# A two-layer diffusion step: the modulation products of VectorE over 512 inputs per instruction instead of 256

## The chip, the cores and the metric

The kernel runs on one core of one Trainium2 chip. Its time is the device time of one execution in microseconds (us); the time before is the median of three runs. The engines of a core are TensorE (PE), VectorE (DVE), ScalarE (ACT), GpSimd (POOL) and SyncE (SP); each works through its own list of instructions in order, and semaphores hold an instruction until what it needs is there.

## The reference, cut to what matters

Two layers run over 640 tokens: 128 context tokens and 512 latent ones, of width 2048. Each layer computes

```
shift, scale, gate = silu(cond) @ ada_w[l] + ada_b[l]     # cond: c_ctx or c, 2048 wide
h   = x * (1 + scale) + shift
z   = h @ w_in[l]                                          # 6656 wide, 52 tiles of 128
mix = [attention * silu(ag), hgrn2 * silu(hgate), silu(LN(conv)) * silu(cgate)]
x   = LayerNorm(ALPHA * x + gate * (mix @ w_out[l]))
```

`cond` is one vector for the context tokens and another for the latent ones, so each of the 3 x 2048 modulation values of a layer is needed twice. The change concerns `silu(cond) @ ada_w`, and in it the four parts that VectorE computes: the gate of layer 0, and scale, shift and gate of layer 1.

## The kernel before, in words

The matrix products run on TensorE in fp32r, with each operand split into a high and a low part. A layer takes the 52 column tiles of `w_in` one after the other (`NTILES`, line 35: 16 tiles of the recurrence, 4 of its gate, 12 of attention, 8 of the convolution (`cb`, `ca`), then 8 of `ag`, tiles 40 to 47, and 4 of `cgate`, tiles 48 to 51). Each tile's product lands in one of two PSUM buffers `z` (the list `ZP`), and is fetched from there by a generator of its own, which hands the buffer back (`zput`). After the tiles come five column groups of `w_out` and the layer norm.

The order of all instructions is written out by the program itself. The loop over the tiles (line 1254) emits the matmuls of a tile in four chunks and calls `pump(3, rate)` twice in each, eight times a tile. `pump` (line 260) adds `rate` to a credit, spends each whole credit on one step of the modulation (`pump_ada`), and then lets the generators in `active` take up to three steps, in the order of the list. A step is what a generator emits up to its next `yield`; one that can't get a buffer yields `BLOCK`, and that counts as no step. The rates of layer 0 are 1.0 for tiles 3 to 19, 0.85 for 20 to 31, 0.5 for 32 to 44 and 1.2 for 45 to 51 (`RATE`, line 74); in the first four groups of `w_out`, twelve pumps each give 4/3. Layer 1 gives 0.5, 0.5, 0.0 and 0.8.

`pump_until(cond)` (line 277) emits until a condition holds: it gives one step to the generators, and when all of them are blocked, one step to the modulation. Before each tile it waits in this way for a free `z` (line 1255); before the last group of `w_out` it waits until no modulation of layer 0 is left (line 1470).

`S` (line 142) is a list of nine scratch buffers of 128 x 688, from which nearly everything takes its working space; a buffer given back goes to the end of the list. Those that matter here:

- `ada_dve` (line 337), the modulation. A part is 8 blocks of 256 inputs; a block takes 8 tiles of weights (128 x 512, `raw`, three of them on the way) and one `S` buffer with both conditioning rows of that block, fetched from `crow` in DRAM and spread over all partitions. The buffer of the next block is taken in the middle of a block (`q == 4`), that of the finished block goes back at its end. One step holds two products of 256 inputs (`dve.scalar_tensor_tensor` with `accum_out`).
- `e_ca` (line 1009 on) leaves the convolution's result of its four tiles in one `S` buffer each.
- `conv_ln` (line 1035), the layer norm over the convolution. It starts when the four results are there and attention is done, takes two buffers (`r`, `r2`), emits sums, waits five steps, and takes two more for each of two column sums (`summed`, line 1050: `hi, lo = yield from S.getn(F32R, F32R)`). It gives the four results and `r2` back after the first column sum, and at its end sets the flags `("mix", l, 12)` to `("mix", l, 15)`.
- `e_gate` (line 1094) takes one buffer, writes silu of its `z` into it, gives `z` back, then waits for the flag of its part of `mix`. For the four `cgate` tiles this is the flag of `conv_ln`.

`getn` (line 112) takes several buffers at once, and takes none until all are free.

Of the kernel before, what the change touches and what calls it, by code (L numbers as in the profile page):

```python
# [9 lines left out]
F32 = mybir.dt.float32  # L10
F32R = mybir.dt.float32r
BF16 = mybir.dt.bfloat16
U8 = mybir.dt.uint8
AF = mybir.ActivationFunctionType
ALU = mybir.AluOpType
AX = mybir.AxisListType

P = 128
D = 2048
KT = 16  # L20
# [52 lines left out]
ADAD = [(0, 2), (1, 1), (1, 0), (1, 2)]  # L73
# [52 lines left out]
def trunk(ctx: ExitStack, tc: tile.TileContext, A: dict):  # L126
    nc = tc.nc
    act, dve, pool, pe, sync = nc.scalar, nc.vector, nc.gpsimd, nc.tensor, nc.sync
# [3 lines left out]
    drp = ctx.enter_context(tc.tile_pool(name="drp", bufs=1, space=bass.MemoryType.DRAM))  # L132
    ctx.enter_context(tc.manual_schedule())

    def new(name, shape, dt=F32):
        return sb.tile(shape, dt, name=name)
# [5 lines left out]
    S = Slots(sb, "s", 9, SLOT)  # L142
# [6 lines left out]
    cmask = new("cmask", [P, 4 * 32], U8)  # L149
    Zd = Slots(sb, "zd", 1, 4 * 160)  # L150
    sm = new("sm", [P, SMW])
    junk = new("junk", [P, 256], BF16)
    aacc = new("aacc", [P, 8, 32])
    nsink = new("nsink", [P, 16])
    oml = new("oml", [P, 2, 4])
    lbt = new("lbt", [P, 2, 2, 4])
# [9 lines left out]
    mb = [psp.tile([P, 512], F32, name=f"m{i}") for i in range(4)]  # L166
    ZP = Free(zt)
    M = Free(mb)
    crow = drp.tile([8, 2, 256], F32, name="crow")
    gsc = drp.tile([2, 2, D], F32, name="gsc")  # L170
    n0 = drp.tile([T, D], F32, name="n0")

# [43 lines left out]
    pool.memset(scs[:, 0:512], 0.0)  # L216
    act.activation(scond[:, :, 0:2], sm[:, SM["cond"]:SM["cond"] + 32].rearrange("p (k c) -> p k c", c=2), AF.Silu)
    crs = S.take()
    sync.dma_start(out=crs[0:16, 0:256], in_=A["condr"])
    act.activation(crs[0:16, 0:256], crs[0:16, 0:256], AF.Silu)  # L220
    pool.dma_start(out=crow.rearrange("a c k -> (a c) k"), in_=crs[0:16, 0:256])
    S.put(crs)

    def zput(z):
# [70 lines left out]
    def adab(l, part):  # L295
        o = SM["adab"] + 48 * l + 16 * part
        return sm[:, o:o + 16]
# [38 lines left out]

    def ada_dve(l, part):
        pi = ADAD.index((l, part))
        rows, fly = deque(), deque()
        tiles = [(kb, q) for kb in range(8) for q in range(8)]  # L340
        nrow = nxt = 0
        for kb, q in tiles:
            while nxt < len(tiles) and len(fly) < (HF if hold else FL):
                if fly and len(RAW.f) <= KEEP[0]:
                    break
                r = yield from RAW.get()
                sync.dma_start(out=r, in_=A["adawD"][pi, tiles[nxt][0], tiles[nxt][1]])
                fly.append(r)
                nxt += 1
            if nrow <= kb or (nrow <= min(kb + 1, 7) and q == 4):  # L350
                t = yield from S.get()
                sync.dma_start(out=t[:, 0:512], in_=crow[nrow].rearrange("c k -> (c k)").partition_broadcast(P))
                rows.append(t)
                nrow += 1
            yield
            r = fly.popleft()
            for n in range(2):
                if n:
                    yield
                for c in range(2):  # L360
                    o = 2 * (2 * q + n) + c
                    dve.scalar_tensor_tensor(junk, r[:, 256 * n:256 * n + 256], 1.0, rows[0][:, 256 * c:256 * c + 256],  # L362
                                             op0=ALU.mult, op1=ALU.mult, accum_out=aacc[:, kb, o:o + 1])
            RAW.put(r)
            if q == 7:
                S.put(rows.popleft())
        yield
        b = adab(l, part).unsqueeze(2).to_broadcast([P, KT, 2])
        t = yield from S.get()
        gT = t[:, 32:64].rearrange("p (c k) -> p c k", c=2)  # L370
        dst = (shf, scl)[part][l] if part < 2 else gT.rearrange("p c k -> p k c")
        dve.tensor_reduce(t[:, 0:32], aacc.rearrange("p a x -> p x a"), axis=AX.X, op=ALU.add)
        dve.scalar_tensor_tensor(dst, t[:, 0:32].rearrange("p (k c) -> p k c", c=2), float(part % 2), b,
                                 op0=ALU.add, op1=ALU.add)
        if part == 2:
            yield
            yield
            yield
            b2 = yield from M.get()
            pe.transpose(b2[0:32, 0:128], t[:, 32:64], ident)  # L380
            act.copy(t[0:32, 128:256], b2[0:32, 0:128])
            M.put(b2)
            act.dma_start(out=gsc[l].rearrange("c (k p) -> (c k) p", p=P), in_=t[0:32, 128:256])
        S.put(t)
        flags.add(("ada", l, part))
# [832 lines left out]
    for l in range(DEPTH):  # L1218
        if l == 0:
            adaq.extend([ada_dve(0, 2), ada_dve(1, 1), ada_dve(1, 0)])  # L1220
        else:
            adaq.append(ada_dve(l, 2))
# [196 lines left out]
        for gi, (n0c, w) in enumerate(GROUPS[:-1]):  # L1419
# [4 lines left out]
            for k0 in range(0, KT, 2):  # L1424
                for tts, k in [(p, k) for p in ((range(3), range(3, TT)) if k0 == 0 else (range(TT),))
                               for k in (k0, k0 + 1)]:
                    hi, lo = osp[l, gi, k // kper]
                    o = w * (k % kper)
# [47 lines left out]
        for tt in range(TT):  # L1476
            b = banks.popleft() if last else obank[tt]
            for k in range(KT):
                hi, lo = osp[l, gi, k // 2]
                o = w * (k % 2)  # L1480
# [50 lines left out]
def pack(i):  # L1531
    f = np.float32
    ac = np.ascontiguousarray
    a = {}
    xs = np.concatenate([i["x_prompt"][0], i["x_sample"][0]], 0)
    a["xr"] = ac(xs)
    a["xT"] = ac(xs.reshape(T, KT, P).transpose(2, 1, 0))
    w = np.asarray(i["w_in"])
    cols = np.concatenate([np.arange(OFF[n] + 128 * j, OFF[n] + 128 * j + 128) for n, j in NTILES])
    w = w[:, :, cols].reshape(DEPTH, 4, 4, P, NN, P)  # L1540
    a["win"] = ac(w.transpose(0, 4, 1, 3, 2, 5)).reshape(DEPTH, NN, 4, P, 512)
    wo = np.asarray(i["w_out"])
    tiles = []
    for n0c, wd in GROUPS:
        kper = 512 // wd
        t = wo[:, :, n0c:n0c + wd].reshape(DEPTH, KT // kper, kper, P, wd)
        tiles.append(t.transpose(0, 1, 3, 2, 4).reshape(DEPTH, KT // kper, P, 512))
    a["wout"] = ac(np.concatenate(tiles, 1))
    aw = np.asarray(i["ada_w"])
    a0 = aw[0].reshape(4, 4, P, 3, 8, 256)[:, :, :, 0:2]  # L1550
    a["adaw0"] = ac(a0.transpose(3, 4, 0, 2, 1, 5)).reshape(2, 8, 4, P, 1024)
    ad = np.stack([aw[l][:, D * p:D * p + D].reshape(8, 256, 8, 2, P) for l, p in ADAD])
    a["adawD"] = ac(ad.transpose(0, 1, 3, 5, 4, 2)).reshape(4, 8, 8, P, 512)
    a["lnw_r"] = ac(i["ln_w"])
    a["lnb_r"] = ac(i["ln_b"])
    a["ckT"] = ac(np.asarray(i["cache_k"])[0].transpose(0, 3, 2, 1)).reshape(DEPTH, P, 256)
    a["cv"] = ac(i["cache_v"][0]).reshape(DEPTH, P, 256)
    a["st"] = ac(np.asarray(i["state_hgrn"])[0].transpose(0, 3, 1, 2, 4))
    s = np.zeros((P, SMW), f)

    def put(n, v):
        v = np.asarray(v).reshape(P, -1)
        s[:, SM[n]:SM[n] + v.shape[1]] = v

    def ch(v, n):
        return np.asarray(v).reshape(DEPTH, n, P).transpose(2, 0, 1)

    put("lb", np.asarray(i["hg_lower_bounds"]).reshape(2, DEPTH, 4, P).transpose(3, 0, 1, 2))
    put("normw", ch(i["hg_norm_w"], 4))
    put("convw", np.asarray(i["conv_w"]).reshape(DEPTH, TAPS, 4, P).transpose(3, 0, 2, 1))  # L1570
    put("convb", ch(i["conv_b"], 4))
    put("clnw", ch(i["conv_ln_w"], 4))
    put("clnb", ch(i["conv_ln_b"], 4))
    put("lnw", ch(i["ln_w"], KT))
    put("lnb", ch(i["ln_b"], KT))
    put("sink", np.broadcast_to(np.asarray(i["attn_sink"]).reshape(1, 16), (P, 16)))
    cond = np.stack([np.asarray(i["c_ctx"]), np.asarray(i["c"])[0]], -1)
    put("cond", cond.reshape(KT, P, 2).transpose(1, 0, 2))
    put("adab", np.asarray(i["ada_b"]).reshape(DEPTH, 3, KT, P).transpose(3, 0, 1, 2))
    a["condr"] = ac(cond.T.reshape(2, 8, 256).transpose(1, 0, 2)).reshape(16, 256)  # L1580
    a["small"] = s
    a["ident"] = np.eye(P, dtype=f)
    p = np.arange(P)
    t = np.arange(512)
    inv = (np.float32(10000.0) ** (-np.arange(32, dtype=f) / np.float32(32))).astype(f)
    pos = np.where((p < 64)[:, None], (t // 64)[None], (t % 64)[None]).astype(f)
    ang = (pos * inv[p % 32][:, None]).astype(f)
    a["cos"] = np.cos(ang).astype(f)
    a["sin"] = (np.sin(ang) * np.where((p % 64) < 32, -1, 1)[:, None]).astype(f)
    m = np.zeros((P, 640), f)  # L1590
    b = np.arange(P)
    m[:, 128:256] = np.where(b[None] >= p[:, None], 0, NEG)
    m[:, 384:512] = np.where(b[None] <= p[:, None], 0, NEG)
    a["amask"] = m
    si = (p % 32)[:, None]
    ti = np.arange(32)[None]
    same16, same8 = (si // 16 == ti // 16), (si // 8 == ti // 8)
    cm = np.stack([~same16, same16 & ~same8, same8 & (ti >= si), same8 & (ti <= si)], 1)
    a["cmask"] = cm.reshape(P, 128).astype(f)
    return a  # L1600
# [20 lines left out]
```

## Time and profile before

| | |
|---|---|
| median of 3 runs | 2241.13 us (2240.1 to 2241.21) |
| the profiled execution | 2247.12 us, span 2245.3 us |
| TensorE busy | 2177.4 us (97%) |
| VectorE busy | 1457.9 us (65%) |
| ScalarE, GpSimd busy | 1144.7 us, 601.9 us |
| mean granted TensorE clock | 0.994 of full speed |

The span runs from the first instruction to the last; the profiled execution is 6 us above the median of the runs. Layer 0 takes the tiles from about 120 to 934 us, then `w_out` to about 1160 us; layer 1 follows in the same way. A busy TensorE is not TensorE at its peak, since matmuls are pipelined and their ends are modelled.

### The profile page before, as it was taken

The numbers are of one execution on the slowest core, as the hardware profiler recorded it, in microseconds if no ns is written. First come the engines' busy times: TensorE is split into PE (matmuls) and PEld (weight loads), VectorE is DVE, ScalarE is ACT, GpSimd is POOL, SyncE is SP. The second block draws the span as 40 slices with busy tenths as digits, with TensorE's granted clock in tenths as the row PEclk, the third lists the DMA queues.
The fourth block names the chain that finished last, engine by engine and source line by source line (L and its number), as shares of the span: only waits on it lengthen the run. The fifth ranks groups of instructions, "written<-read, shape, count | busy, mean of one in ns | idle before, by whom it ended". The sixth has DMA issues, their size and how long they took to land.

```text
span 2245.3 us, 42128 instructions
## 1 busy us (share of the span) xinstructions
PE 2177.4 (97%) x15854; PEld 2076.1 (92%) x15854; DVE 1457.9 (65%) x3799; ACT 1144.7 (51%) x2051; POOL 601.9 (27%) x690
## 2 busy tenths in 40 slices
PE   5899999999999999999989999999999999999997
PEld 2699999999999999988989999999999999998887
DVE  2478899557669999766673666543654779225457
ACT  1267877546565435511155787774555543462112
POOL 0033344332222343300032344433222123331003
PEclk9999999999999999999999999999999999999999
DMA  9978787897766888964426777778776576676333
GB/s 358 392 206 199 185 209 182 201 219 173 176 159 155 206 193 212 259 233 128 128 108 158 156 172 162 162 173 189 160 163 137 110 173 147 150 164 212 99 99 123
DMA packets 210557, 403.61 MB, mean 180 GB/s; under 512 B 24656, under 2 KB 30512, under 8 KB 209712
## 3 DMA queue, kind: packets, MB, share of 16 engines
q1 hardware_dynamic: 138992, 271.85, 38.4%
q0 software_dynamic: 61440, 116.96, 30.2%
q10 hardware_dynamic: 9920, 12.10, 1.7%
q8 instruction: 124, 2.03, 0.4%
q14 instruction: 81, 0.66, 0.1%
HBM read 383.46 MB, written 12.11 MB: 176 GB/s over the span
## 4 chain that ended last, share of the span: by engine, by line
PE 75%; DVE 9%; DMA 6%; issue 5%; ACT 3%; POOL 1%; ACTq 1%; SPq 0%; POOLq 0%; DVEq 0%
PE z L1175 29%; PE z L1173 19%; PE z L1431 9%; PE m L1431 8%; DVE junk L362 4%; DMA x<-adaw 2%; PE m L948 2%; PE m L1482 2%; PE m L862 1%; DMA s<-xT 1%; PE m L916 1%; DMA s<-s 1%; DMA wh<-win 1%; PE m L664 1%; ACT s L1391 1%
## 5 line engine op out<-in xcount | busy, mean ns | idle before, releaser
L1175 PE MATMUL z<-HH,wh 128*128 128x384 f32 x3296 | 1046.6, 339 | 0.0
L1173 PE MATMUL z<-HH,wh 128*128 128x256 f32 x3296 | 926.6, 283 | 1.9 <-DMA wh<-win 1.0
L292 POOL DMA_DIRECT2D wh<-win x388 | 345.2, 936 | 1095.3 <-ACT wh L291 1024.0
L1173 PEld LDWEIGHTS z<-HH,wh 128*128 128x128 f32 x3296 | 619.5, 189 | 5.8 <-DVE wh L287 1.6
L1175 PEld LDWEIGHTS z<-HH,wh 128*128 128x128 f32 x3296 | 620.6, 188 | 1.5
L1175 PE MATMUL z<-HL,wh 128*128 128x384 f32 x1648 | 558.2, 339 | 0.0
L362 DVE SCALAR_TENSOR_TENSOR junk<-raw,s 128x256 bf16<-128x256 f32 x1024 | 502.5, 491 | 53.2 <-DMA raw<-adawD 25.0
L1173 PE MATMUL z<-HL,wh 128*128 128x256 f32 x1648 | 461.6, 280 | 0.0
L1173 PEld LDWEIGHTS z<-HL,wh 128*128 128x128 f32 x1648 | 310.9, 189 | 0.0
L1175 PEld LDWEIGHTS z<-HL,wh 128*128 128x128 f32 x1648 | 310.4, 188 | 0.0
L291 ACT ACTIVATE wh<-wh 128x512 fp32r<-128x512 f32 x400 | 253.0, 633 | 78.5 <-PE z L1175 67.4
L290 ACT CAST wh<-raw 128x512 fp32r<-128x512 f32 x400 | 244.0, 610 | 72.0 <-issue 36.1
L286 ACT CAST wh<-raw 128x512 fp32r<-128x512 f32 x136 | 83.0, 621 | 305.0 <-PE m L1431 153.8
L1027 DVE SCALAR_TENSOR_TENSOR s<-s,sm,s 128x655 f32<-128x655 f32 x240 | 229.6, 957 | 6.3
L1431 PE MATMUL z<-wh,HH 128*128 128x512 f32 (+1 forms) x640 | 182.1, 368 | 0.0
L1431 PE MATMUL m<-wh,HH 128*128 128x512 f32 (+1 forms) x640 | 173.8, 357 | 0.0
L287 DVE TENSOR_TENSOR wh<-raw,wh 128x512 fp32r<-128x512 f32 x138 | 92.6, 687 | 119.5 <-ACT wh L286 119.5
L1431 PEld LDWEIGHTS z<-wh,HH 128*128 128x128 f32 x640 | 116.1, 189 | 20.1
L1431 PEld LDWEIGHTS m<-wh,HH 128*128 128x128 f32 x640 | 114.2, 189 | 17.6
L1431 PE MATMUL z<-wh,HL 128*128 128x512 f32 (+1 forms) x320 | 117.8, 368 | 0.0
L1431 PE MATMUL m<-wh,HL 128*128 128x512 f32 (+1 forms) x320 | 114.4, 358 | 0.0
L1096 ACT ACTIVATE s<-z 128x640 f32<-128x640 f32 x32 | 22.5, 703 | 152.5 <-PE z L1175 143.7
(561 smaller groups left out, 2718.6 us busy)
## 6 DMA issues: line engine op xcount, KB each, us to landing
raw<-win SPq DMA_DIRECT2D x416, 256.0 KB, 4.2
wh<-win POOLq DMA_DIRECT2D x388, 256.0 KB, 5.6
raw<-adawD SPq DMA_DIRECT2D x256, 256.0 KB, 4.2
x<-adaw SPq DMA_DIRECT2D x64, 512.0 KB, 8.3
raw<-wout SPq DMA_DIRECT2D x128, 256.0 KB, 2.7
s<-crow SPq DMA_DIRECT2D x32, 256.0 KB, 5.9
s<-xT ACTq DMA_DIRECT2D x16, 320.0 KB, 7.5
s<-s ACTq DMA_DIRECT2D x80, 64.0 KB, 3.9
```

Of the source, the lines that this page charges most:

```text
L286: act.copy(hi, src)
L287: (lo_eng or dve).tensor_tensor(lo, src, hi.bitcast(F32), op=ALU.subtract)
L290: act.copy(hi, r)
L291: act.activation(lo, hi.bitcast(F32), AF.Copy, scale=-1.0)
L292: pool.dma_start(out=lo, in_=w.bitcast(F32R), accum_op=ALU.add)
L362: dve.scalar_tensor_tensor(junk, r[:, 256 * n:256 * n + 256], 1.0, rows[0][:, 256 * c:256 * c + 256], op0=ALU.mult, op1=ALU.mult, accum_ou ...
L948: pe.matmul(o, lhsT=v_, rhs=p_, start=(y == 0 and n_ == 0), stop=(y == len(bl) - 1 and n_ == 2))
L1027: dve.scalar_tensor_tensor(acc, u[:, t:t + AW], sm[:, cw + t:cw + t + 1], acc, op0=ALU.mult, op1=ALU.add)
L1173: pe.matmul(za, lhsT=w_, rhs=h_[:, 0:2, k, :], start=st_, stop=sp_)
L1175: pe.matmul(zb, lhsT=w_, rhs=h_[:, 2:5, k, :], start=st_, stop=sp_)
L1431: pe.matmul(bs[tt][:, 0:w], lhsT=h_[:, tt, k, :], rhs=w_[:, o:o + w], start=(k == 0 and n_ == 0), stop=(k == KT - 1 and n_ == 2))
L1482: pe.matmul(b[:, 0:w], lhsT=h_[:, tt, k, :], rhs=w_[:, o:o + w], start=(k == 0 and n_ == 0), stop=(k == KT - 1 and n_ == 2))
```

## The change

VectorE's products run over 512 inputs instead of 256, so a part is 4 blocks of 16 weight tiles of 512 inputs x 128 outputs. The two conditioning rows of a block no longer fit into one buffer of `S`; they are taken together, as two buffers, at the start of a block, and both go back at its end, after which the next block takes its two. There is one more `yield` at the start of each block. A step now holds one product of 512 inputs. The host packs the weights and the conditioning rows to match, and the partial sums `aacc` have 4 x 32 columns instead of 8 x 32.

```diff
-    junk = new("junk", [P, 256], BF16)
-    aacc = new("aacc", [P, 8, 32])
+    junk = new("junk", [P, 512], BF16)
+    aacc = new("aacc", [P, 4, 32])
...
-    crow = drp.tile([8, 2, 256], F32, name="crow")
+    crow = drp.tile([4, 2, 512], F32, name="crow")
...
     def ada_dve(l, part):
         pi = ADAD.index((l, part))
-        rows, fly = deque(), deque()
-        tiles = [(kb, q) for kb in range(8) for q in range(8)]
-        nrow = nxt = 0
+        fly = deque()
+        tiles = [(kb, q) for kb in range(4) for q in range(KT)]
+        nxt = 0
         for kb, q in tiles:
             while nxt < len(tiles) and len(fly) < (HF if hold else FL):
...
                 nxt += 1
-            if nrow <= kb or (nrow <= min(kb + 1, 7) and q == 4):
-                t = yield from S.get()
-                sync.dma_start(out=t[:, 0:512], in_=crow[nrow].rearrange("c k -> (c k)").partition_broadcast(P))
-                rows.append(t)
-                nrow += 1
-            yield
+            if q == 0:
+                rows = yield from S.getn(F32, F32)
+                for c in range(2):
+                    sync.dma_start(out=rows[c][:, 0:512], in_=crow[kb, c].partition_broadcast(P))
+                yield
             r = fly.popleft()
-            for n in range(2):
-                if n:
-                    yield
-                for c in range(2):
-                    o = 2 * (2 * q + n) + c
-                    dve.scalar_tensor_tensor(junk, r[:, 256 * n:256 * n + 256], 1.0, rows[0][:, 256 * c:256 * c + 256],
-                                             op0=ALU.mult, op1=ALU.mult, accum_out=aacc[:, kb, o:o + 1])
+            for c in range(2):
+                yield
+                o = 2 * q + c
+                dve.scalar_tensor_tensor(junk, r, 1.0, rows[c][:, 0:512], op0=ALU.mult, op1=ALU.mult,
+                                         accum_out=aacc[:, kb, o:o + 1])
             RAW.put(r)
-            if q == 7:
-                S.put(rows.popleft())
+            if q == KT - 1:
+                S.put(*rows)
         yield
```

## Rows read from the trace of the kernel before

**Rows 1.** The page: busy us of each engine, its share of the span, instructions.
```profile
PE 2177.4 (97%) x15854; PEld 2076.1 (92%) x15854; DVE 1457.9 (65%) x3799; ACT 1144.7 (51%) x2051; POOL 601.9 (27%) x690
```
**Rows 2.** Waits of PE, 120 to 420 us: us in total, times, longest.
```profile
PE m L540 <- DVE s L534: 4.5, 4, 1.4
PE m L540 <- DVE s L607: 3.2, 4, 1.3
```
**Rows 3.** Windows: length, busy us by engine (instructions), PE clock, DMA share, GB/s.
```profile
200.00:240.00 40.00, 38.65 (x354) 38.12 (x353) 36.55 (x89) 32.23 (x47) 18.16 (x17) 1.00 0.77 184
...
520.00:560.00 40.00, 37.79 (x259) 37.26 (x258) 30.07 (x113) 24.29 (x61) 9.69 (x11) 0.96 0.76 174
```
**Rows 4.** The page, groups: busy us, mean ns of one, idle before it, releaser.
```profile
L362 DVE SCALAR_TENSOR_TENSOR junk<-raw,s 128x256 bf16<-128x256 f32 x1024 | 502.5, 491 | 53.2 <-DMA raw<-adawD 25.0
```
**Rows 5.** Timeline of DVE: start us, us, line, operation, idle before it.
```profile
208.02 0.42 DVE L362 SCALAR_TENSOR_TENSOR junk<-raw,s 128x256 bf16<-128x256 f32 x1
...
210.82 0.42 DVE L362 SCALAR_TENSOR_TENSOR junk<-raw,s 128x256 bf16<-128x256 f32 x1
...
1096.29 0.69 DVE L1337 SCALAR_TENSOR_TENSOR y0y<-y0y,z 128x512 f32<-128x512 f32 x1
...
1125.42 0.42 DVE L1337 SCALAR_TENSOR_TENSOR y0y<-y0y,m 128x256 f32<-128x256 f32 x1
```
**Rows 6.** Timeline of DVE and POOL, 223 to 230 us.
```profile
223.70 6.16 DVE L362 SCALAR_TENSOR_TENSOR junk<-raw,s 128x256 bf16<-128x256 f32 x1
...
227.87 1.69 POOL L524 TENSOR_TENSOR s<-h01gg 128x640 f32<-128x640 f32 x1
```
**Rows 7.** Windows of line 362 alone: length, DVE busy (instructions), clock, DMA.
```profile
120.00:920.30 800.30, 338.05 (x1275) 1.00 0.80 192
```
**Rows 8.** Timeline of ACT: silu of the last two tiles' z, layer 0.
```profile
920.33 0.71 ACT L1096 ACTIVATE s<-z 128x640 f32<-128x640 f32 x1 [6.83 <-PE z L1175]
...
934.35 0.70 ACT L1096 ACTIVATE s<-z 128x640 f32<-128x640 f32 x1 [4.47 <-PE z L1175]
```
**Rows 9.** Timeline of SP: the third load of w_out in layer 0.
```profile
914.92 0.46 SPq L1147 DMA_DIRECT2D raw<-wout  x1
```
**Rows 10.** Line 352, the loads of the rows: time from issue to landing.
```profile
DMA to landing us min/median/max: 3.0/5.9/10.9
```
**Rows 11.** Timeline of ACT, DVE and POOL: what conv_ln issues in layer 0.
```profile
853.97 0.73 ACT L286 CAST s<-s 128x640 fp32r<-128x640 f32 x1 [4.21 <-DVE junk L362]
...
862.23 0.29 DVE L1068 SCALAR_TENSOR_TENSOR a00k<-m,s 128x128 f32<-128x128 f32 x1 [0.25 <-PE m L427]
...
865.35 0.42 DVE L1068 SCALAR_TENSOR_TENSOR a01v<-m,s 128x256 f32<-128x256 f32 x1
...
866.26 1.74 POOL L1046 TENSOR_TENSOR s<-s,s 128x640 f32<-128x640 f32 x1 [6.56 <-ACT s L1072]
...
882.18 0.95 ACT L1080 ACTIVATE s<-m,eps 128x384 f32<-128x384 f32 x2 [2.45 <-PE m L427]
883.14 1.28 ACT L1082 ACT_TABLE_LOAD   x1
884.43 0.74 ACT L1082 ACTIVATE s<-s 128x640 f32<-128x640 f32 x1
...
886.21 0.82 DVE L1085 TENSOR_TENSOR a00k<-a00k,s 128x640 f32<-128x640 f32 x1
...
890.12 0.91 ACT L1091 ACTIVATE a01v<-a01v,sm 128x640 f32<-128x640 f32 x1
```
**Rows 12.** Waits of DVE, whole run: us in total, times, longest.
```profile
DVE a11k L1103 <- ACT s L1096: 32.5, 1, 32.5
```
**Rows 13.** Timeline of DVE where layer 0 ends.
```profile
1131.63 0.19 DVE L1352 TENSOR_TENSOR scl<-scl,sm 128x32 f32<-128x32 f32 x1
...
1137.91 0.43 DVE L1336 TENSOR_TENSOR z<-z,s 128x256 f32<-128x256 f32 x1 [2.35 <-PE z L1482]
```

More of the change, by code (lines that the diff above doesn't have):

```diff
@@ L218, in trunk @@
     crs = S.take()
-    sync.dma_start(out=crs[0:16, 0:256], in_=A["condr"])
-    act.activation(crs[0:16, 0:256], crs[0:16, 0:256], AF.Silu)
-    pool.dma_start(out=crow.rearrange("a c k -> (a c) k"), in_=crs[0:16, 0:256])
+    sync.dma_start(out=crs[0:8, 0:512], in_=A["condr"])
+    act.activation(crs[0:8, 0:512], crs[0:8, 0:512], AF.Silu)
+    pool.dma_start(out=crow.rearrange("a c k -> (a c) k"), in_=crs[0:8, 0:512])
     S.put(crs)
@@ L1551, in pack @@
     a["adaw0"] = ac(a0.transpose(3, 4, 0, 2, 1, 5)).reshape(2, 8, 4, P, 1024)
-    ad = np.stack([aw[l][:, D * p:D * p + D].reshape(8, 256, 8, 2, P) for l, p in ADAD])
-    a["adawD"] = ac(ad.transpose(0, 1, 3, 5, 4, 2)).reshape(4, 8, 8, P, 512)
+    ad = np.stack([aw[l][:, D * p:D * p + D].reshape(4, 512, KT, P) for l, p in ADAD])
+    a["adawD"] = ac(ad.transpose(0, 1, 3, 4, 2))
     a["lnw_r"] = ac(i["ln_w"])
@@ L1579, in pack @@
     put("adab", np.asarray(i["ada_b"]).reshape(DEPTH, 3, KT, P).transpose(3, 0, 1, 2))
-    a["condr"] = ac(cond.T.reshape(2, 8, 256).transpose(1, 0, 2)).reshape(16, 256)
+    a["condr"] = ac(cond.T.reshape(2, 4, 512).transpose(1, 0, 2)).reshape(8, 512)
     a["small"] = s
```

## The prediction

> **What bounds the kernel now.** First the busy shares: TensorE stands at 97% of the span, VectorE at 65% [rows 1]. A faster VectorE can only pay where TensorE waits for it, so the second view is TensorE's waits. In layer 0's recurrence there are eight, all for `lev_mul` and `base_mul` (lines 534 and 607), 7.7 us together [rows 2]. The windows show why: from 200 to 240 us VectorE is busy 36.6 of 40 us [rows 3]. That is nearly all the change can win. The products are VectorE's costliest group, 1024 of them in 502.5 us [rows 4], but elsewhere they lie beside a TensorE that is full anyway. The third thing to read is no view: the order of the instructions is written out by generators that share nine buffers, and the change alters how the modulation holds them. I count that through in the code, with times from the trace.
>
> **The product itself.** Six products of 256 inputs take 2.80 us from start to start, 0.467 each with the accumulator's read [rows 5]. The same operation without an accumulator takes 0.42 us for 256 columns and 0.69 for 512 [rows 5], so 256 more columns cost 0.27 us, and a product of 512 should take 0.467 + 0.27 = 0.74 us. A step had two products (0.93 us) and will have one: 0.2 us less. Over the four parts, 512 x 0.2 = 100 us of VectorE go.
>
> What of it TensorE sees: at most the 7.7 us [rows 2]. A head has four tiles, 32 steps, so its VectorE work shrinks by 6.4 us, but part of the delay isn't work: a product that runs into GpSimd's subtractions stands for 6.16 us and ends just after them, 227.87 + 1.69 = 229.56 [rows 6]. I take half, a gain of 4 us (bounds 0 and 7.7).
>
> [...]
>
> **The buffers.** Before, a block held one of the nine `S` buffers, and a second one from its middle on. After, a block holds two throughout. At its end it gives both back, and in the same step, with no `yield` between, the next block takes two; no other generator can get in. Only at the end of a part is there a `yield` after the buffers go back.
>
> Now `conv_ln` of layer 0. It holds four results, `r` and `r2`: six. With two rows that makes eight. Its next call needs two at once, and one is left. Before, one row was held at that moment: seven, two left, and it went on. After the change it stays blocked until the modulation part that is running ends.
>
> How far is that part? Before, a part had 129 steps (132 for a gate); after, 4 x 33 + 1 = 133 (136). Layer 0's parts are gate, scale, shift, so the third begins with step 270 and gives its rows back at step 402. The credits up to the end of tile 50 are 17 x 8 x 1.0 + 12 x 8 x 0.85 + 13 x 8 x 0.5 + 6 x 8 x 1.2 = 327 steps. (The trace agrees with this counting: 1275 instructions of line 362 by 920.3 us [rows 7], four to a step, are 319 steps with products; the rest are steps without any, and a few lost ones.) So `conv_ln` stands from tile 46 on, with 75 steps to go when tile 50 is through.
>
> Then TensorE stops. `e_gate` of tile 48 takes the ninth buffer and waits for `conv_ln`'s flag. `e_gate` of tile 49 finds none and can't fetch its `z`; tile 50 holds the other. Before tile 51, `pump_until` finds every generator blocked and emits modulation steps, one after another, until step 402: 73 products and two changes of block. `conv_ln`, first in the list, then gets every single step until its end; only after it does tile 49's `z` come free.
>
> The price, along the path: TensorE is through with tile 50 at 920.3 us [rows 8]. VectorE has nothing but products to do by then, held back by SP's queue, which loads their tiles in turn with the weights; SP passes the last load of tile 50's turn at 914.9 us [rows 9], so I let the burst begin at 915 (bounds 905, if SP gets there earlier with fewer waits, and 921). It takes 73 x 0.74 = 54 us. At both changes of block the only free buffers are the two just given back, so SP can load the new rows only after the last product; that is a landing time, median 5.9, from 3.0 to 10.9 [rows 10], and I take 5 us twice, nearer the lower end because little else is loading then (bounds 6 and 22). VectorE is done at 915 + 54 + 10 = 979.
>
> The rest of `conv_ln` then runs with nothing between: two splits (0.73 + 0.82 each) 3.1, twelve products with the mean from 862.23 to 865.77, 3.5, the last square 0.7, new sums 1.7 + 0.8, logarithm 0.95, a table load and the exponential 1.3 + 0.7, four products 3.0, the last silu 0.9 [rows 11] (shapes that stand there once are used again), silu of tile 49's `z` 0.7 [rows 8]. That is 17.4; with two column sums and some ten hand-overs I take 21. Below stands 17.4, above the 37 us from 853.97 to 891.03 that the stretch takes today with modulation in between [rows 11]. TensorE goes on at 1000: 79.5 us lost.
>
> TensorE's clock: the window with 2.2 us of idle TensorE is granted 0.96 instead of 1.00 [rows 3], that is 1.6 us; I add 1.6 for the restart (bounds 0 and 3). [...]
>
> **What lies beside other work.** Layer 1 blocks in the same way, but there the part gives its rows back at its step 133, 120 steps are done by tile 31 (30 x 8 x 0.5), and tiles 45 and 46 give 12.8 more, so the buffers are free by about the end of tile 46 and no `z` is held. `conv_ln` comes at most a tile or two later, and VectorE stands 32.5 us before the gate of tile 50 there [rows 12]; I count 0, and up to 5 if that cover is thinner. The 64 steps that used to run beside `w_out` are gone from there, which gains nothing, since TensorE is full. Row loads elsewhere are issued two steps ahead of use instead of eight; SP runs ahead of VectorE, so 0, at worst a few us of VectorE. The smaller reduction at the end of a part saves tenths.
>
> Sum: 79.5 + 1.6 - 4 = +77 us. The profiled execution's 2247.1 becomes 2324; the median of the runs lies 6 us lower, 2241.1, and becomes **2318 us**. With all bounds low: 905 + 54 + 6 + 17.4 - 920.3 = 62, less 7.7, gives 2295; all high: 921 + 54 + 22 + 37 - 920.3 = 114, plus 3, gives 2358.
>
> **The rivals.** *Not slower: `conv_ln` finds its two buffers.* If it gets in at any change of block before tile 51, nothing stops TensorE. For it: the list is shared, and before the change `conv_ln` passed with none to spare. Against it: giving back and taking stand in one step, and blocked generators keep no claim. The time then: the 4 us gained, against twelve more steps in layer 0. There 400.8 credits meet 391 steps and three lost ones, so seven are spare and five steps are left over; they are emitted before the last group of `w_out` (5 x 0.74 = 3.7 us), at 1131.6, where VectorE has 2.35 us of slack at 1137.91 [rows 13] and TensorE waits for the norm next: +1.4 to +3.7. That makes about 2239, between 2233 and 2245. The point from which it decides: two free buffers at one pump between tiles 46 and 51.
>
> *Half rate.* If a further column costs twice what rows 5 say, 0.54 us for 256, a product takes 1.0 us, the burst 73 us instead of 54, and the gain in the recurrence goes: 2241 + 98.5 + 1.6 = 2341. [...]
>
> **How the numbers follow.** The forecast 0.88, the first rival 0.08 (half of it faster, half the same), half rate 0.04. The range 2296 to 2350 leaves out the first rival, the last us of the low bounds and the corner where all bounds are high, together 2 in 10. About 0.2% (4.5 us) is what a measurement can tell from no change: faster 0.04, same 0.04, slower 0.92.
>
> **What would show it.** A pause of TensorE of 60 to 110 us before layer 0's last tile, at about 920 us; in it a dense row of products of 512 with two gaps of some 5 us, then `conv_ln`'s lines without products between, then line 1096 and the tile; products at 0.74 us from start to start; none of them beside layer 0's `w_out`; lines 534 and 607 shorter in TensorE's waits. Wrong would be the whole step if `conv_ln`'s first split (853.97 before) comes ahead of the products of step 402, and the sizes if the gaps or the chain after the burst lie outside their bounds.

## The result and the profile after

The changed kernel takes 2313.26 us (median of four runs, 2312.59 to 2319.98) against 2240.88 us for the kernel before (four runs, 2240.1 to 2241.21): 1.033 times as long, 95% interval 1.0311 to 1.035. That is 72 us slower; the forecast was 77 us, 2318 us. The profiled execution took 2312.59 us, with a span of 2310.7 us. Behind `ada_dve` each line number is 3 lower than before (`zsb(z)`'s silu is L1093, `conv_ln`'s squares L1069).

The page of the changed kernel, part 1 (answers to [rows 1]), then two of its slice rows (tenths of 40 slices), then the group of the products (answers to [rows 4]):

```profile
PE 2183.9 (95%) x15854; PEld 2080.7 (90%) x15854; DVE 1368.9 (59%) x2775; ACT 1144.2 (50%) x2051; POOL 605.0 (26%) x690
...
PE   6899999999999997099998999999999999999997
...
PEclk9999999999999998599999999999999999999999
...
L359 DVE SCALAR_TENSOR_TENSOR junk<-raw,s 128x512 bf16<-128x512 f32 x512 | 400.4, 782 | 58.5 <-DMA s<-crow 35.7
```

VectorE's products did get cheaper: 400.4 us instead of 502.5, 102 us saved where 100 were counted. TensorE's busy time is the same within 0.3%, but one slice in the middle of the run holds a zero, and the granted clock there drops to about half. The waits of PE over the whole run (us in total, times, longest) name it:

```profile
PE m L423 <- ACT s L286: 63.3, 2, 55.6
...
PE z L1170 <- ACT s L1093: 8.3, 2, 7.9
PE m L537 <- DVE s L604: 3.2, 2, 1.7
```

and PE's timeline shows the place (start, us, idle before it; the last matmul of tile 50 ends at 907.7, the first of tile 51 is L1170):

```profile
963.28 0.69 PE L423 MATMUL m<-s,ones 128*128 128x384 f32 x1 [55.57 <-ACT s L286]
...
972.98 0.69 PE L423 MATMUL m<-s,ones 128*128 128x384 f32 x1 [7.73 <-ACT s L286]
...
982.87 0.58 PE L1170 MATMUL z<-HH,wh 128*128 128x256 f32 x1 [7.91 <-ACT s L1093]
```

For 75.2 us TensorE has nothing but the column sums of `conv_ln` (L423, L424). What VectorE does meanwhile, from its timeline (the accumulator's reads are left out by "..."):

```profile
902.03 0.69 DVE L359 SCALAR_TENSOR_TENSOR junk<-raw,s 128x512 bf16<-128x512 f32 x1 [1.13 <-DMA raw<-adawD]
...
902.76 0.69 DVE L359 SCALAR_TENSOR_TENSOR junk<-raw,s 128x512 bf16<-128x512 f32 x1
...
911.99 0.69 DVE L359 SCALAR_TENSOR_TENSOR junk<-raw,s 128x512 bf16<-128x512 f32 x1 [2.49 <-DMA s<-crow]
...
939.24 0.69 DVE L359 SCALAR_TENSOR_TENSOR junk<-raw,s 128x512 bf16<-128x512 f32 x1 [2.92 <-DMA s<-crow]
```

From 902.03 to 963.1 us it computes the 55th to the 128th product of the third part in one row, 0.733 us from start to start, with two gaps where it waits for new rows. Of the 327 steps of the prediction 58 belong to this part, three of them without a product, so the 55th still comes out beside tile 50; the 73 that are emitted ahead of tile 51 begin with the 56th, at 902.76 us. SP issues each row when VectorE is done with its buffer, the first as the last product of the block begins (908.80), the second when that ends:

```profile
908.79 1.06 SPq L353 DMA_DIRECT2D s<-crow  x2
```

ScalarE's timeline (answers to [rows 11, 8]) shows who waited for the last products, and the chain that follows:

```profile
962.50 0.72 ACT L286 CAST s<-s 128x640 fp32r<-128x640 f32 x1 [63.57 <-DVE junk L359]
...
972.20 0.72 ACT L286 CAST s<-s 128x640 fp32r<-128x640 f32 x1 [2.15 <-DVE s L1045]
...
974.57 0.95 ACT L1077 ACTIVATE s<-m,eps 128x384 f32<-128x384 f32 x2 [0.34 <-PE m L424]
...
982.13 1.27 ACT L1093 ACTIVATE s<-z 128x640 f32<-128x640 f32 x2
```

The first cast is `conv_ln`'s first split, 109 us later than before (853.97 in [rows 11]); it starts when the last product but one, the last that reads the first row's buffer, is done. The last line is the silu of tiles 49 and 50, which frees `z`. Last, the windows around the restart (length, busy us by engine, PE clock, DMA share, GB/s):

```profile
908.00:963.00 55.00, 0.00 (x0) 0.00 (x0) 46.02 (x133) 0.50 (x1) 0.00 (x0) 0.52 0.61 176
963.00:983.00 20.00, 3.74 (x9) 2.35 (x9) 11.68 (x24) 13.22 (x18) 3.79 (x3) 0.50 0.08 25
983.00:988.00 5.00, 5.00 (x19) 5.00 (x20) 1.70 (x1) 4.87 (x9) 3.99 (x4) 0.50 0.50 109
988.00:993.00 5.00, 5.00 (x33) 5.00 (x32) 3.10 (x5) 3.07 (x7) 0.93 (x2) 0.91 1.08 244
993.00:1000.00 7.00, 7.00 (x49) 6.96 (x49) 1.90 (x3) 1.45 (x4) 0.00 (x0) 1.00 0.27 49
```

Tile 51 begins at a granted clock of 0.50 and costs 5 x 0.50 + 5 x 0.09 = 3.0 us more than at full clock.

### The profile page after: what moved, and what is told of

Same layout as the page of the kernel before. It is cut to its first block, busy times and chain, and to the rows that moved or that the text cites. A ratio compares the mean times of both kernels' runs of the same rounds, so it can differ in the third digit from the quotient of the medians.

```text
span 2310.7 us, 41189 instructions
## 1 busy us (share of the span) xinstructions
PE 2183.9 (95%) x15854; PEld 2080.7 (90%) x15854; DVE 1368.9 (59%) x2775; ACT 1144.2 (50%) x2051; POOL 605.0 (26%) x690
## 3 DMA queue, kind: packets, MB, share of 16 engines
q1 hardware_dynamic: 138976, 271.85, 37.6%
## 4 chain that ended last, share of the span: by engine, by line
PE 79%; issue 5%; DMA 5%; DVE 5%; ACT 3%; POOL 3%; ACTq 0%; SPq 0%; POOLq 0%; DVEq 0%
PE z L1172 32%; PE z L1170 21%; PE z L1428 9%; PE m L1428 8%; DMA x<-adaw 2%; DVE junk L359 2%; PE m L945 2%; PE m L859 2%; PE m L1479 1%; PE m L913 1%; DMA raw<-adawD 1%; DMA s<-xT 1%; POOL s L521 1%; POOL s L518 1%; DMA s<-crow 1%
## 5 line engine op out<-in xcount | busy, mean ns | idle before, releaser
L1170 PE MATMUL z<-HH,wh 128*128 128x256 f32 x3296 | 927.9, 283 | 8.5 <-ACT s L1093 8.3
L1170 PEld LDWEIGHTS z<-HH,wh 128*128 128x128 f32 x3296 | 621.4, 189 | 12.1 <-ACT s L1093 8.8
L1170 PE MATMUL z<-HL,wh 128*128 128x256 f32 x1648 | 462.4, 281 | 0.0
L359 DVE SCALAR_TENSOR_TENSOR junk<-raw,s 128x512 bf16<-128x512 f32 x512 | 400.4, 782 | 58.5 <-DMA s<-crow 35.7
L1170 PEld LDWEIGHTS z<-HL,wh 128*128 128x128 f32 x1648 | 311.9, 189 | 0.0
L1093 ACT ACTIVATE s<-z 128x640 f32<-128x640 f32 x32 | 22.4, 703 | 130.4 <-PE z L1172 130.3
```

What stands on the lines that cost most here:

```text
L359: dve.scalar_tensor_tensor(junk, r, 1.0, rows[c][:, 0:512], op0=ALU.mult, op1=ALU.mult, accum_out=aacc[:, kb, o:o + 1])
L1170: pe.matmul(za, lhsT=w_, rhs=h_[:, 0:2, k, :], start=st_, stop=sp_)
```

## The experiments

Seven more kernels were run, and the kernel before a second time. The theory: with two rows held from block to block, `conv_ln` is starved of buffers, and the modulation's remaining steps are emitted ahead of layer 0's last tile. The rivals: the wide product, or its pairs of rows, stop TensorE there by themselves; and the gain in the recurrence is scatter. The table has, for the profile of each kernel, the us between the starts of the last matmuls of two tiles of layer 0; its first two rows are the kernel before, and the "first" of them is the profile of [rows 1 to 13]. The first three tiles of layer 0 run interleaved, so tile 0 ends late, at 122 to 124 us. A tile beside nothing special takes 14.08 us (50 to 51 before). The medians were taken beside 2240.88 us for the kernel before (the changed kernel), 2241.94 (experiments 1 to 4) and 2241.05 (5 to 7). The 5.7 us that some of the expectations give for the recurrence were counted from about 68 us, when the interleaved tiles are still under way; from the end of tile 0 the same two profiles differ by 6.2.

| kernel | tiles 0 to 17 | 24 to 26 | 50 to 51, over 14.08 | 51 to next layer's 0 | median, us |
|---|---|---|---|---|---|
| before, first profile | 258.7 | 39.7 | 0 | 259.3 | 2240.88 |
| before, profiled again | 259.2 | 35.9 | 0 | 260.2 | 2241.83 (one run) |
| changed | 252.5 | 37.6 | 78.1 | 260.3 | 2313.26 |
| changed, `r2` given back | 252.5 | 39.7 | 0 | 259.3 | 2237.71 |
| changed, yield at the block's end | 253.2 | 35.6 | 0.6 | 275.0 | 2248.33 |
| before, two rows held | 259.6 | 35.9 | 76.3 | 259.3 | 2318.21 |
| changed, narrow products | 259.2 | 42.6 | 90.6 | 260.0 | 2336.51 |
| changed, rate 1.4 | 252.5 | 48.5 | 34.3 | 259.3 | 2284.08 |
| narrow products, `r2` given back | 259.3 | 40.5 | 0 | 262.6 | 2249.29 |
| `r2` given back, no products in 25, 26 | 252.5 | 35.6 | 0 | 260.3 | 2236.59 |

**1. `conv_ln` gives back `r2`.** In the changed kernel:

```diff
-        def summed():
+        def summed(give):
+            S.put(*give)
             hi, lo = yield from S.getn(F32R, F32R)
...
-        bs = yield from summed()
+        bs = yield from summed([r2])
+        r2 = S.take()
```

(the second call gives nothing back).

> The changed kernel, with one edit in conv_ln: it hands its scratch buffer r2 back in the same step in which it takes the two buffers of the first column sum, and takes one again after it. It then needs seven buffers at most where it needed eight, and seven and the two rows make nine. Theory (starved buffers): conv_ln is never blocked, no modulation steps are emitted ahead of layer 0's last tile, and TensorE has no pause over 3 us there. Of the 72.4 us between the two medians everything but the gain goes: 2240.9 less the six us that TensorE waits less for lev_mul and base_mul in the changed kernel, plus 0 to 2 us for two steps left over before the last group of w_out: 2235 to 2238 us. Rival (the wide products or the loads of two rows at once stop TensorE at that place by themselves): the pause stays, 2290 to 2315 us. Second rival (nothing is won in the recurrence, the shorter waits are one execution's scatter): no pause, 2240 to 2243 us.

Measured: 2237.71 us against 2241.94 beside it, ratio 0.9983 (0.9974 to 0.9992). The window that holds the pause of the changed kernel is full:

```profile
908.00:960.00 52.00, 52.00 (x273) 45.99 (x272) 31.15 (x65) 25.41 (x44) 13.20 (x21) 1.00 0.95 291
```

The products, the rows, their pairs and the loads are all those of the changed kernel; one buffer fewer in `conv_ln` and the loss is gone, 75.5 us of it between the two medians. The rival that products or rows stop TensorE by themselves falls. The second rival, 2240 to 2243, falls too, though the gain is only 4 us.

**2. One yield between giving back and taking.** In the changed kernel:

```diff
             if q == KT - 1:
                 S.put(*rows)
+                if kb < 3:
+                    yield
```

> The changed kernel, with one more yield in ada_dve: between giving back the two rows of a block and taking the two of the next. Theory (starved buffers): conv_ln, blocked since tile 46, gets its two at the first change of block, in tile 49; no pause of TensorE over 3 us before layer 0's last tile. Six steps of modulation are refused while conv_ln holds the buffers and there are twelve more steps in layer 0, so 17 are left over before the last group of w_out: 17 x 0.733 = 12.5 us of VectorE, of which some 2 us have cover. 2235 to 2238 without them, with them 2240 to 2250 us. Rival (the wide products or the loads of the rows stop TensorE by themselves): the pause stays, 2290 to 2325 us.

Measured: 2248.33 us, ratio 1.0027 (1.0017 to 1.0038), in the expected 2240 to 2250. The pause is gone although the modulation holds two buffers as before: it was the taking in the same step that kept `conv_ln` out. The 17 steps left over show as PE's wait at the norm, 10.3 us, where 12.5 less some 2 of cover were counted (us in total, times, longest):

```profile
PE m L1383 <- DVE y0y L1372: 10.3, 1, 10.3
```

The whole stretch from tile 51 to the next layer takes 15.7 us longer than in experiment 1 (275.0 against 259.3). Of the 5.4 us beyond the wait, 2.0 are two waits at the first matmuls of `w_out` (L1430, 1.0 us each), which experiment 1 doesn't have, and some 2 are the clock: the window from 1140 to 1145 us, behind the long wait, was granted 0.53. The expectation had no term for either.

**3. Two buffers held, products of 256.** In the kernel before:

```diff
-            if nrow <= kb or (nrow <= min(kb + 1, 7) and q == 4):
+            while nrow <= min(kb + 1, 7):
...
-                    dve.scalar_tensor_tensor(junk, r[:, 256 * n:256 * n + 256], 1.0, rows[0][:, 256 * c:256 * c + 256],
+                    dve.scalar_tensor_tensor(junk, r[:, 256 * n:256 * n + 256], 1.0, rows[kb == 7][:, 256 * c:256 * c + 256],
...
-            if q == 7:
+            if q == 7 and kb != 6:
                 S.put(rows.popleft())
...
+        S.put(*rows)
```

> The kernel before, products of 256 inputs as they were; the only edit: the modulation holds two buffers of S all through a part (the rows of the next block are taken at the start of a block instead of its middle, and those of the last two blocks go back together at the end). Theory (starved buffers; the width has nothing to do with the loss): conv_ln blocks from tile 46, and 63 steps are emitted ahead of layer 0's last tile, 63 x 0.933 = 58.8 us, begun 5.7 us before TensorE stops; no waits at the changes of block, as rows come a block ahead; then 19.7 us of conv_ln and 3.0 us for the clock, as in the changed kernel: 2240.9 + 58.8 - 5.7 + 19.7 + 3.0 = 2317 us, from 2305 to 2325. Rival (the wide products or rows loaded in pairs make the loss): 2238 to 2246 us.

Measured: 2318.21 us (2315.45 to 2318.87), ratio 1.0336 (1.0322 to 1.035). No product is wide, and the loss is there: 76.3 us at tile 51, where 75.8 were worked out. The cause is how the buffers are held and taken, two at a time from block to block, and not the width. PE's waits:

```profile
PE m L427 <- ACT s L286: 48.2, 2, 40.6
...
PE m L428 <- DVE s L287: 14.6, 2, 14.4
...
PE z L1174 <- ACT s L1097: 7.9, 1, 7.9
```

**4. The changed kernel with narrow products.**

```diff
-                dve.scalar_tensor_tensor(junk, r, 1.0, rows[c][:, 0:512], op0=ALU.mult, op1=ALU.mult,
-                                         accum_out=aacc[:, kb, o:o + 1])
+                for n in range(2):
+                    m_ = slice(256 * n, 256 * n + 256)
+                    dve.scalar_tensor_tensor(junk, r[:, m_], 1.0, rows[c][:, m_], op0=ALU.mult, op1=ALU.mult,
+                                             accum_out=aacc[:, 2 * kb + n, o:o + 1])
```

> The changed kernel with its blocks of 512 inputs, two rows in two buffers and all steps as they are; but each product of 512 inputs is done as two of 256 (0.467 us each from start to start instead of one of 0.733). It tells what the width by itself is worth. Theory: the burst before layer 0's last tile is 73 x 0.2 = 14.6 us longer, and the 5.7 us in the recurrence are lost again: 2313.3 + 14.6 + 5.7 = 2334 us, from 2326 to 2340. Rival (wide products hurt, by rate or by the shared work of GpSimd): not slower than 2313 us. Second rival (the gain in the recurrence is scatter): 2313.3 + 14.6 = 2328 us, with waits for lev_mul and base_mul as short as in the changed kernel.

Measured: 2336.51 us, ratio 1.0421 (1.0406 to 1.0435), in the expected 2326 to 2340. The loss at tile 51 grows by 12.5 us (14.6 expected), and the waits in the recurrence are back (PE, 120 to 420 us):

```profile
PE m L539 <- DVE s L533: 4.9, 4, 1.3
PE m L539 <- DVE s L606: 3.3, 4, 1.4
```

So the width itself helps in both places; the half rate of the rival in the prediction, 1.0 us a product, is not there (0.733 us in the changed kernel). The rest of the 23 us lies in tiles 0 to 17 (6.7 by the table) and at tiles 24 to 26 (5.0, below).

**5. Fewer steps left.** In the changed kernel:

```diff
-RATE = ((1.0, 0.85, 0.5, 1.2), (0.5, 0.5, 0.0, 0.8))
+RATE = ((1.0, 1.4, 0.5, 1.2), (0.5, 0.5, 0.0, 0.8))
```

> The changed kernel with one number other: the modulation's rate in tiles 20 to 31 of layer 0 is 1.4 instead of 0.85. The third part is then 52 steps further when tile 50 is through: 23 steps are emitted ahead of layer 0's last tile instead of 75, and no change of block is among them. Theory (conv_ln waits until the part ends, so the loss is a sum: steps left x 0.733 us, plus the changes of block, plus conv_ln's rest and the clock): the row of products shrinks from 61.1 to 23 x 0.733 = 16.9 us, TensorE's idle time there from 71 to 27 us, the time from 2313.3 to 2269 us; up to 10 us more if VectorE, with 39 us more products in the attention tiles, holds up TensorE there: 2265 to 2280. Rival (a loss that doesn't hang on the number of steps left, such as rows, loads or a restart): 2300 to 2320 us.

Measured: 2284.08 us, ratio 1.0191 (1.0177 to 1.0205), outside the 2265 to 2280 of the theory and far from the rival's 2300 to 2320. The term in question came out: the loss at tile 51 fell by 43.8 us, where 44.2 were worked out. That it fits to 0.4 us is luck: TensorE's stop fell by 42.4 us (75.16 to 32.72), mostly since the 23 products took 18.2 us and not 16.9, and the restart happened to cost 1.4 us less. What was too low is the price of the products in the attention tiles, 10.9 us at tiles 24 to 26 and 2.5 later, against "up to 10". PE's waits show it:

```profile
PE m L859 <- DVE ats L874: 6.9, 2, 4.0
```

**6. The control for the gain.** Experiment 1 with the narrow products of experiment 4.

> The kernel in which conv_ln hands back r2, with each product of 512 inputs done as two of 256. It is the control for the gain: the same steps, rows and buffers as r2_given_back, without the wide product. Theory (the gain comes from the width): the eight waits for lev_mul and base_mul are back, 8 us together in layer 0, and the time is that of the kernel before or a little above, for two more steps: 2240 to 2247 us, 3 to 9 us above r2_given_back. Rival (the gain of r2_given_back comes from conv_ln's new handling or the new order of the loads): 2235 to 2239 us.

Measured: 2249.29 us, ratio 1.0038 (1.0024 to 1.0052), 11.6 us above experiment 1 and so 2 us outside what was expected. In the profiles 6.8 us of them are in the recurrence, where the eight waits stand again (4.9 and 3.3 us), 0.8 at tiles 24 to 26, and 3.3 at the layer's end, where TensorE now waits 1.4 us for the norm, more than the expectation gave the two steps left over. The gain is the width's, not `conv_ln`'s new handling.

**7. No products in tiles 25 and 26.** Experiment 1 with

```diff
+            if l == 0 and i in (25, 26):
+                rate = 0.0
```

and a rate of 0.64 instead of 0.5 in tiles 32 to 44.

> r2_given_back, and no modulation steps in tiles 25 and 26 of layer 0; the 14 steps are made up for by a rate of 0.64 instead of 0.50 in tiles 32 to 44. In r2_given_back TensorE waits 2.2 us at 514.5 us for the attention's reduction (line 874), which stands behind two products in VectorE's list, and the granted clock is 0.84 and 0.91 in the 14 us around it: 2.2 + 0.16 x 7 - ... together some 2 to 4 us. Theory: with no products there the wait and the dip go, 2233 to 2236 us. Rival (the wait is the attention's own, or comes up at another tile, or VectorE has no room in tiles 32 to 44): 2237 to 2245 us.

Measured: 2236.59 us, ratio 0.9977 (0.9968 to 0.9986), between the theory's 2236 and the rival's 2237, so the time decides for neither. The wait for `ats` is gone from the profile and tiles 24 to 26 take 4.1 us less; but the medians of the two kernels are 1.1 us apart and their intervals overlap. It beats both kernels of this study; that it beats experiment 1 is not shown.

**8. The kernel before, profiled again.**

> The kernel before, unchanged, profiled a second time: its first profiled execution took 2247.1 us, 6 us above the median of its runs, so the step by step comparison with it is uncertain by as much. Theory: the eight waits for lev_mul and base_mul stand there again, 7 to 9 us together, so that what the changed kernel wins in the recurrence, 5.7 us by the first profile, is no scatter; the 6 us above the median are elsewhere (before the first tile, or at the attention's wait in tile 26). Rival: the waits are shorter in an execution near the median, 2 to 4 us together.

Measured: 2241.83 us. The eight waits are there, 5.0 and 3.1 us (PE, 120 to 420 us), so the gain is no scatter. What the first profile has and this one hasn't is the wait in tile 26. The same stretch (519 to 533 us, the columns as above) in this kernel's two profiles, the first, then the second:

```profile
519.00:526.00 7.00, 4.79 (x33) 4.55 (x32) 6.58 (x21) 3.11 (x9) 2.16 (x2) 0.94 0.68 107
526.00:533.00 7.00, 7.00 (x41) 7.00 (x41) 6.11 (x25) 4.86 (x11) 1.53 (x2) 0.81 0.71 185
```

```profile
519.00:526.00 7.00, 6.95 (x51) 6.71 (x50) 5.99 (x22) 4.24 (x10) 1.74 (x2) 1.00 0.55 122
526.00:533.00 7.00, 7.00 (x54) 7.00 (x54) 5.75 (x27) 3.35 (x10) 1.43 (x2) 1.00 0.82 207
```

## Why the prediction was right

The mechanism came as described; the sizes, step by step:

| step of the prediction | said | measured |
|---|---|---|
| a product of 512, start to start | 0.74 us | 0.733 us |
| products emitted ahead of tile 51 | 73, two changes of block | 73, two changes |
| the 73 products begin, against TensorE's stop | 5.3 us ahead (915 to 920.3) | 4.9 us (902.76 to 907.7) |
| a change of block | 5 us (3 to 11) | 3.4 us |
| products and changes together | 64 us | 60.4 us |
| rest of `conv_ln` and the silu | 21 us (17.4 to 37) | 19.7 us (963.15 to 982.87) |
| TensorE's stop | 79.5 us | 75.2 us |
| clock | 1.6 us (0 to 3) | 3.0 us |
| gain in the recurrence | 4 us (0 to 7.7) | 6.2 to 6.7 us |

**The stop** is 4.3 us shorter than said. Most of that is the row loads. At 5 us a change I stood nearer the low end of [rows 10] because little else is loading there (in the changed kernel the DMA share is 1.00 from 900 to 908 us and 0.47 from 908 to 912), and not near enough: between the last product of a block and the first of the next 3.19 and 3.62 us pass from start to start, and a little more before the second row's product (0.9 and 0.5); less one product's 0.733, that is 3.4 us each. The rest of `conv_ln` takes 19.7 us in all four profiles that have the stop; three table loads of 1.28 us are in it, where the prediction counted one. Two slips change nothing: 915 + 54 + 10 + 21 - 920.3 is 79.7 and not 79.5, and the steps that used to run beside `w_out` are 57 and not 64 (114 products of the kernel before start behind its tile 51).

**The gain** was taken as half of TensorE's eight waits, on the ground that a product held up by GpSimd doesn't get shorter. It is nearly all of them: 7.7 us before, 1.7 after, by the waits of PE from 120 to 420 us in the changed kernel:

```profile
PE m L537 <- DVE s L604: 1.7, 1, 1.7
```

By the table, tiles 0 to 17 take 252.5 to 253.2 us in the five profiles with wide products and 258.7 to 259.6 in the five with narrow ones. The argument about GpSimd was the step that failed, and not because such products cost little. From 120 to 420 us, 13 of the 263 products of the kernel before take over 1 us more than the shortest, 41 us in all; in the changed kernel it is 6 of 132, 26 us (12 to 14 in the five narrow profiles, 6 or 7 in the five wide ones). In both kernels each of them ends 0.3 to 0.6 us after an operation of GpSimd does. With half as many products, half as many are held up, so this time shrinks too. How much of the gain comes from it, and how much from the shorter work, no run here separates. What the timed runs keep of the gain is less, 4.2 us in experiment 1. In its profile 3.8 us of the gain are given back at tile 26, where that execution meets the attention's wait and the second one of the kernel before doesn't. How often a kernel meets it was not measured.

**The clock** stands at the upper bound. The prediction's 1.6 us come from a window with 2.2 us of idle TensorE [rows 3] and stand there for a stop of some 80; that the longer stop costs the restart no more was the author's estimate, and no row of the kernel before shows it. In the runs the stop of 75 us cost 3.0 us afterwards; in experiment 4 an idle time of 3.60 us at tile 26 cost 7 x (0.12 + 0.37) = 3.4 us, by the windows below (519 to 533 us). The other long stops, of 88, 74 and 33 us (experiments 4, 3 and 5), cost tile 51 2.4, 1.9 and 1.6 us, by the table's column less the stop, so 3.0 is not a fixed price.

```profile
519.00:526.00 7.00, 3.40 (x23) 2.90 (x22) 6.66 (x22) 3.27 (x11) 2.90 (x3) 0.88 0.62 129
526.00:533.00 7.00, 7.00 (x34) 7.00 (x34) 6.00 (x24) 4.86 (x12) 0.95 (x2) 0.63 0.80 184
```

**What was not in the sum:** `conv_ln`'s eight column-sum matmuls, 3.6 us at a granted clock of 0.50, run inside the stop instead of between the matmuls of the tiles before. From tile 46 to tile 50 the four profiles with the stop take 56.3 us, the six without it 56.9 to 58.5.

Together, against the second profile of the kernel before: 78.1 at tile 51, less 1.3 before the end of tile 0, less 6.7 in tiles 0 to 17, plus 1.6 at tiles 24 to 26, less 2.1 from tile 46 to 50 (0.7 of it a wait of TensorE that only the kernel before shows there), and 1.0 in smaller steps: 70.6 us at layer 1's last tile, and 70.8 between the two profiled executions. The medians say 72.4.

**Layer 1** cost nothing, as counted: from layer 0's last tile to layer 1's last the changed kernel takes as long as the one before, to 0.5 us. VectorE's cover at tile 50 there fell from 32.5 us [rows 12] to this (waits of DVE in the changed kernel):

```profile
DVE a11k L1100 <- ACT s L1093: 23.1, 1, 23.1
```

**Products gone from beside `w_out`** gained nothing, as said: 260.3 us from tile 51 to the next layer's first, against 259.3 and 260.2.

**The rivals.** *`conv_ln` finds its two buffers* did not happen, but its point of decision was the right one: one yield at a change of block is enough (experiment 2), and steps left over at the norm do cost, a wait of 10.3 us for 17. *Half rate*: 512 columns take 0.69 us and 256 take 0.42 [rows 5], with the accumulator as without. The prediction took the price from line 1337, one of whose fp32 sources lies in PSUM; the product of 512, with both fp32 sources in `raw` and `S`, takes the same 0.69 us. The 256 further columns cost 0.27 us and not the rival's 0.54.

## What to carry to other kernels

Where generators share a list of buffers, a change of how many are held, and for how long, has to be counted against the holder with the highest peak before any instruction is priced: here 8 + 2 against 9 cost 78 us, and a saving of 102 us on an engine off the path brought 4. A request for several buffers at once starves beside one that gives back and takes again in the same step; a yield between the two, or one buffer fewer in the one that waits, settles it (2248.3 and 2237.7 us). And a forced emission shows in the trace as one dense row of a single line beside an idle TensorE: its length is steps left x spacing (23 x 0.733 = 16.9 us against 18.2 in experiment 5), plus the waits for loads.

## What was not expected of the hardware

The granted clock did not answer every short wait. After TensorE waits in tile 26 for `ats`, the windows around are these (512 to 519 and 519 to 526 us): in the changed kernel, after 1.67 us of idle,

```profile
512.00:519.00 7.00, 5.33 (x40) 5.09 (x39) 5.96 (x15) 4.60 (x13) 1.70 (x3) 1.00 0.65 143
519.00:526.00 7.00, 7.00 (x54) 7.00 (x53) 6.10 (x20) 3.88 (x12) 2.16 (x3) 1.00 0.82 202
```

and in experiment 1, after 2.24 us,

```profile
512.00:519.00 7.00, 4.75 (x29) 4.52 (x28) 6.18 (x18) 4.41 (x11) 1.83 (x2) 0.84 0.63 122
519.00:526.00 7.00, 7.00 (x47) 7.00 (x46) 6.44 (x21) 4.60 (x13) 2.31 (x3) 0.91 0.77 215
```

The second wait is 0.6 us longer and costs 7 x (0.16 + 0.09) = 1.8 us more in clock. Nor did the length alone give the price. In experiment 6, after 3.06 us of idle at the same place, the windows from 519 to 533 us are

```profile
519.00:526.00 7.00, 3.94 (x26) 3.70 (x25) 6.12 (x22) 4.31 (x11) 1.52 (x2) 0.90 0.57 129
526.00:533.00 7.00, 7.00 (x44) 7.00 (x43) 6.53 (x28) 4.70 (x13) 2.12 (x3) 0.85 0.69 174
```

and cost 7 x (0.10 + 0.15) = 1.8 us, as much as after the 2.24 us in experiment 1, and half of the 3.4 after 3.60 us in experiment 4. The order of VectorE's instructions at that place is the same in the changed kernel and in experiment 1; why one execution waits 2.2 us there and another of the same kernel not at all is open.
